# Latent attention with two passes over v, division ahead of the transposes, and column parts in turn

## The chip, the cores and the metric

One core of a Trainium2 chip runs the whole program. The metric is device time in microseconds (us), from the runs of the kernel; beside it stands one profiled execution, from which all details come. The core has a matrix engine (TensorE, PE in the profile, with its weight loads as PEld), a vector engine (VectorE, DVE), a scalar engine (ScalarE, ACT), a general engine (GpSimd, POOL) and a queue that issues transfers (SyncE, SP). The matrix engine writes to PSUM, whose 2 KB banks hold 512 float32 columns; the rest lives in SBUF.

## The reference

Four layers work on 512 latent tokens and 256 context tokens, each 1024 wide. The layers' token mixers are, in order: Fourier mixing, differential attention, latent attention (MLA) and Fourier mixing. Each is followed by a dense layer of 4096 squared-ReLU units. Each sub-layer is preceded by an RMS norm with shift and scale and followed by a gate. After the second layer only the latent stream is updated, so that the third and fourth layers compute 512 columns where the first two compute 768.

```python
def mla_attend(q_nope, q_rope, k_nope, k_rope, v):
    scale = (MLA_NOPE_DIM + MLA_ROPE_DIM) ** -0.5
    s = (jnp.einsum("bqhd,bkhd->bhqk", q_nope, k_nope)
         + jnp.einsum("bqhr,bkr->bhqk", q_rope, k_rope)).astype(jnp.float32) * scale
    p = jax.nn.softmax(s, axis=-1)
    return jnp.einsum("bhqk,bkhe->bqhe", p.astype(v.dtype), v)
...
def sq_relu_mlp(h, w1, w2):
    return jnp.square(jax.nn.relu(h @ w1)) @ w2
```

The latent attention has 16 heads of 64 + 32 (rotary) for the scores and 64 for the values; its queries come from a normalised compression of 256, keys and values from one of 128, and all heads share one rotary key. Each of the 512 latent queries attends to 768 keys.

## The kernel before

All is float32. A product of two float32 operands is made of three matmuls: each operand is split into a high part, rounded for the matrix engine, and a low part, the rest (`split`, L95: ACT copies, DVE subtracts), and high by high, high by low and low by high are added in PSUM. `mm3g` (L147) is that product over k tiles. In it the column parts are the innermost loop: with 768 columns each pair of operands is used for 512 columns and then, at once, for 256 or 258.

**Dense layers** (`mlp`, L394). Per layer there are 32 units `w1(m)` (L413): one load of 128 x 1024 weights, a product over eight k tiles with all columns, and squared ReLU. After each four units comes `w2(j)` (L439): output products over four k tiles for the eight rows of x, accumulated into x by DVE (`accum`, L368, with priority 200). The norm's factor is not applied to the operand: h holds x times the scale (high and low), two more columns hold the shift, and DVE multiplies each unit's result by the factor `r_all` while ACT adds the shift's product `bt`. For 512 tokens the columns are cut into 256 and 256 + 2. While a layer runs, DVE makes the next layer's modulation sums (`mod_unit`, L257).

**Latent attention** (`mla`, L1056). First the three compressions, their norms (`lat_norm`, L1092) and the rotary key (`kr_part`, L1126) are made. The PSUM has two buffers `s` of 1024 columns and four `u` of 512. The loop runs over 32 chunks c: half a head's queries, two row tiles i of 128 queries. For a row tile `S(i)` (L1242) makes 128 x 768 scores, DVE the maximum, and ACT the exponential `e`. `Tr(i)` (L1259) transposes e in two groups of three blocks through a `u` buffer each; each group is split (ACT copies to `pth`, DVE subtracts to `ptl`). `PV(c)` (L1267) multiplies by v: 18 matmuls of 256 columns (v high by `pth`, v low by `pth`, v high by `ptl`), where `vt` holds 64 columns of v beside 64 columns of ones, so that the other 64 rows of the result are the row sums; ACT makes their reciprocal (Ln, then Exp) and DVE multiplies. S runs two row tiles ahead of Tr.

Between the row tiles `fill` (L1232) takes items from a queue, each with a written cost in ns: projections of the next heads (`v_item`, `k_item`, `q_item`, `qr_item`) and output products `wo_item` (L1206), eight for each group of two head pairs, six matmuls of 512 columns each, and one accumulation into x. The rotary parts of q and k are copied to their place under the other 64 rows by ACT and DVE (`kk_rope`, L1143; `q_item`, L1193). Weight splits are ACT's and DVE's (`wload`, L99; `gload`, L111). The last group's output products close the layer, each followed by `MlpNorm.feed` (L341): two scaled copies for the dense layer, and a square that POOL adds to `nacc`.

The order on the matrix engine is the program's order (L48). On the other engines a planner sets the order from estimated costs and priorities. Every engine's queue is served in order.

## Time and profile before

| | |
|---|---|
| runs | 2914.56, 2922.34, 2925.98 us, median 2922.34 |
| profiled execution | 2923.1 us, of which the span from first to last instruction is 2921.0 |
| PE, PEld | 2774.7 us (95%), 2443.5 us (84%) |
| DVE, ACT, POOL | 1949.3 us (67%), 1296.0 us (44%), 159.8 us (5%) |
| mean granted clock of the matrix engine | 0.982 |
| DMA | 291.30 MB, mean 100 GB/s |

Busy times overlap within an engine: a matmul's row covers its whole way through the array, and the next one starts before it ends. Where a text says how far apart two matmuls are, it means their starts. The first dense layer runs from about 178 to 700 us, the second from 1221 to 1742, latent attention from 1758 to 2103, the third dense layer from there to 2452, and the fourth from 2553 to 2900. "Idle before" in a group is the time in which its engine did nothing ahead of its instructions, and the name behind it is what ended that.

### The profile page before, as it was taken

The numbers are of one execution on the slowest core, as the hardware profiler recorded it, in microseconds if no ns is written. First come the engines' busy times: TensorE is split into PE (matmuls) and PEld (weight loads), VectorE is DVE, ScalarE is ACT, GpSimd is POOL, SyncE is SP. The second block draws the span as 40 slices with busy tenths as digits, with TensorE's granted clock in tenths as the row PEclk, the third lists the DMA queues.
The fourth block names the chain that finished last, engine by engine and source line by source line (L and its number), as shares of the span: only waits on it lengthen the run. The fifth ranks groups of instructions, "written<-read, shape, count | busy, mean of one in ns | idle before, by whom it ended". The sixth has DMA issues, their size and how long they took to land.

```text
span 2921.0 us, 42412 instructions
## 1 busy us (share of the span) xinstructions
PE 2774.7 (95%) x16875; PEld 2443.5 (84%) x16875; DVE 1949.3 (67%) x3468; ACT 1296.0 (44%) x2309; POOL 159.8 (5%) x172
## 2 busy tenths in 40 slices
PE   8999999999799898899999998899899999999998
PEld 5788888888788777688888896788799898899997
DVE  8986656558687778874555458888776656544454
ACT  4542222234475656433222246777534335543342
POOL 0100000002110010100000010000100001100001
PEclk9999999999899999999999999999999999999999
DMA  9454333232111111343333211010265541232231
GB/s 326 145 173 131 113 110 108 101 106 71 47 48 45 40 48 44 101 158 114 112 122 108 80 37 37 17 37 23 98 212 168 175 148 55 92 104 94 80 109 51
DMA packets 93542, 291.30 MB, mean 100 GB/s; under 512 B 10624, under 2 KB 14880, under 8 KB 92832
## 3 DMA queue, kind: packets, MB, share of 16 engines
q1 hardware_dynamic: 90784, 285.44, 29.5%
q0 software_dynamic: 2560, 3.15, 0.5%
q8 instruction: 133, 2.18, 0.3%
q14 instruction: 65, 0.53, 0.1%
HBM read 283.29 MB, written 2.11 MB: 98 GB/s over the span
## 4 chain that ended last, share of the span: by engine, by line
PE 79%; DVE 13%; ACT 4%; DMA 2%; issue 1%; POOL 1%; POOLq 0%; SPq 0%; ACTq 0%; DVEq 0%
PE pw L140 69%; PE pu L140 5%; PE ps L140 3%; PE pu L770 1%; DVE x L371 1%; DVE ptl L97 1%; DVE mx L921 1%; DVE hlo L330 1%; DVE nu L328 1%; DMA raw<-in_modw 1%; DVE wlo L97 1%; DVE mx L1253 1%; ACT e L1256 1%; PE pn L140 0%; POOL nacc L357 0%
## 5 line engine op out<-in xcount | busy, mean ns | idle before, releaser
L96 ACT CAST whi<-raw 128x1024 fp32r<-128x1024 f32 (+1 forms) x322 | 312.3, 985 | 1059.7 <-PE pw L140 1010.4
L371 DVE SCALAR_TENSOR_TENSOR x<-pw,mod,x 128x512 f32<-128x512 f32 (+1 forms) x504 | 302.6, 623 | 322.1 <-PE pw L140 321.2
L140 PE MATMUL pw<-hhi,wlo 128*128 128x512 f32 (+1 forms) x2112 | 501.9, 314 | 12.3 <-DVE wlo L97 12.3
L140 PE MATMUL pw<-hhi,whi 128*128 128x512 f32 (+1 forms) x2112 | 502.1, 314 | 5.3 <-ACT whi L96 3.6
L140 PE MATMUL pw<-hlo,whi 128*128 128x512 f32 (+1 forms) x2112 | 501.8, 314 | 0.0
L140 PE MATMUL pw<-ahi,wlo 128*128 128x512 f32 (+1 forms) x1664 | 500.0, 344 | 0.0
L140 PE MATMUL pw<-ahi,whi 128*128 128x512 f32 (+1 forms) x1664 | 496.6, 342 | 0.3 <-DVE x L371 0.3
L140 PE MATMUL pw<-alo,whi 128*128 128x512 f32 (+1 forms) x1664 | 494.9, 341 | 0.0
L97 DVE TENSOR_TENSOR wlo<-raw,whi 128x1024 fp32r<-128x1024 f32 (+1 forms) x322 | 361.6, 1139 | 43.5 <-ACT whi L96 39.0
L140 PEld LDWEIGHTS pw<-hhi,wlo 128*128 128x128 f32 x2112 | 332.6, 190 | 36.4 <-DVE wlo L97 13.0
L140 PEld LDWEIGHTS pw<-hhi,whi 128*128 128x128 f32 x2112 | 333.7, 190 | 32.9 <-ACT whi L96 4.0
L140 PEld LDWEIGHTS pw<-hlo,whi 128*128 128x128 f32 x2112 | 332.6, 190 | 23.4
L140 PEld LDWEIGHTS pw<-ahi,whi 128*128 128x128 f32 x1664 | 284.1, 189 | 41.4 <-DVE x L371 0.8
L140 PEld LDWEIGHTS pw<-ahi,wlo 128*128 128x128 f32 x1664 | 282.7, 189 | 36.6
L140 PEld LDWEIGHTS pw<-alo,whi 128*128 128x128 f32 x1664 | 281.1, 188 | 38.0
L264 DVE SCALAR_TENSOR_TENSOR raw<-raw,cb 128x1024 f32<-128x1024 f32 x176 | 216.0, 1228 | 93.0 <-DMA raw<-in_modw 91.3
L97 DVE TENSOR_TENSOR alo<-r,ahi 128x768 fp32r<-128x768 f32 (+2 forms) x134 | 105.9, 793 | 85.5 <-ACT ahi L96 85.3
L431 ACT ACTIVATE r<-r,bt 128x512 f32<-128x512 f32 (+1 forms) x196 | 119.1, 640 | 78.9 <-DVE r L427 78.9
L264 DVE SCALAR_TENSOR_TENSOR junk<-raw,cb 128x1024 bf16<-128x1024 f32 x96 | 117.2, 1221 | 50.7 <-DMA raw<-in_modw 47.6
L420 DVE COPY bt<-pw 128x2 f32<-128x2 f32 x128 | 20.2, 158 | 195.3 <-PE pw L140 195.1
L307 POOL TENSOR_TENSOR nacc<-nacc,nsq 128x256 f32<-128x256 f32 x70 | 52.9, 755 | 1766.2 <-ACT nsq L306 1765.9
L97 DVE TENSOR_TENSOR ptl<-pu,pth 128x384 fp32r<-128x384 f32 (+1 forms) x208 | 106.3, 540 | 37.4 <-ACT pth L96 35.8
(322 smaller groups left out, 4277.9 us busy)
## 6 DMA issues: line engine op xcount, KB each, us to landing
raw<-in_w SPq DMA_DIRECT2D x252, 512.0 KB, 3.8
raw<-in_modw SPq DMA_DIRECT2D x176, 512.0 KB, 3.4
wm<-in_msh SPq DMA_DIRECT2D x32, 256.0 KB, 6.0
raw<-in_fw SPq DMA_DIRECT2D x10, 512.0 KB, 4.6
cb<-scr SPq DMA_DIRECT2D x4, 1024.0 KB, 4.5
raw<-in_dwk SPq DMA_DIRECT2D x16, 256.0 KB, 2.6
raw<-in_dwq SPq DMA_DIRECT2D x16, 256.0 KB, 2.8
raw<-in_dwv SPq DMA_DIRECT2D x16, 256.0 KB, 2.7
```

The costliest lines, as they stand in the source:

```text
L96: nc.scalar.copy(hi, src)
L97: nc.vector.tensor_sub(lo, src, rd(hi))
L140: r = nc.tensor.matmul(o, lhsT, rhs, start=start, stop=stop)
L264: nc.vector.scalar_tensor_tensor(o, m, 1.0, cb[:, v * 1024:(v + 1) * 1024], op0=ALU.mult, op1=ALU.mult, accum_out=mcol(mod[l, ch], v, k))
L307: nc.gpsimd.tensor_tensor(nacc[:, c0:c0 + w], nacc[:, c0:c0 + w], s, op=ALU.add)
L328: nc.vector.scalar_tensor_tensor(u, xs, am, r, op0=ALU.mult, op1=ALU.mult)
L330: nc.vector.scalar_tensor_tensor(lo, u, sh, rd(hi), op0=ALU.add, op1=ALU.subtract)
L371: nc.vector.scalar_tensor_tensor(xs, src, mcol(mod[l, ch], 0 if c0 < SL else 1, n), xs, op0=ALU.mult, op1=ALU.add)
L431: nc.scalar.activation(r[:, c0:c1], r[:, c0:c1], AF.Relu, bias=bt[:, v:v + 1])
L770: nc.tensor.transpose(t[:, i * 128:(i + 1) * 128], p[:, (k0 + i) * 128:(k0 + i + 1) * 128], ident)
L921: nc.vector.reduce_max(mx, sv, axis=AX.X, negate=True)
L1253: nc.vector.reduce_max(mx, s[:, :T], axis=AX.X)
```

## The change

In `mm3g` and `lin_part` the loop over column parts becomes the outer one: all products of the first part, then all of the next.

In the dense layers of 512 tokens, units from the sixth on (`late`) use an h that has been normalised meanwhile: `normed(k)` makes x times scale times `r_all`, plus the shift, and splits it again into the same tiles, while the first block of output products runs. These units take 24 matmuls of 512 columns in place of 48 of 256 and 258, and ACT applies ReLU straight from PSUM; the multiplication by `r_all` and the copy `bt` are gone.

In the latent attention:

- `vt` holds 64 columns of v's high part beside 64 of its low part. PV has two passes, `pth` and `ptl`, of six matmuls each; the two halves of the result are added.
- The division comes first: ACT's exponential also gives the row sum, DVE its reciprocal, and POOL multiplies the 128 x 768 tile. The scale of the scores goes into the query norm's factor `qg`.
- Six transposes fill one tile `t` of 1024 columns, of which there is one, and it is split 768 wide. `u` has two buffers. S runs three row tiles ahead (`LEAD`).
- The rotary parts are moved by transfers on SP's queue.
- Output products take four head pairs at once, 12 matmuls each; the first half's stand in the loop's last half, the second half's at the end, where the first four are made for three pairs ahead of and behind the last PV, and the fourth pair is added after. Their weights, and those of later projections, are split by ACT and POOL (`sub=`).
- At the start k and v are projected and normalised ahead of q; the four rotary key tiles are all made ahead of the loop. The costs in `fill` differ by quarter.

```diff
     def mm3g(o, n, wfn, afn, parts, off=0):
-        for k in range(n):
-            (wh, wl), (ah, al) = wfn(k), afn(k)
-            for i, (w, v) in enumerate(((wh, ah), (wh, al), (wl, ah))):
-                for c0, w_ in parts:
+        for c0, w_ in parts:
+            for k in range(n):
+                (wh, wl), (ah, al) = wfn(k), afn(k)
+                for i, (w, v) in enumerate(((wh, ah), (wh, al), (wl, ah))):
                     mm(o[:, c0 - off:c0 - off + w_], w, v[:, c0:c0 + w_],
                        k == 0 and i == 0, k == n - 1 and i == 2)
                     yield cost(w_)
...
+            wide = T == SL
+            late = CH + 1 if wide else FF
...
+                if m >= late:
+                    mm3(p, KT, lambda k: kview(w, k), lambda k: h[k], [(0, T)])
+                    step = 256 if m == CH * NJ - 1 else T
+                    for o in range(0, T, step):
+                        s = slice(o, o + step)
+                        nc.scalar.activation(r[:, s], p[:, s], AF.Relu)
+                        nc.scalar.activation(r[:, s], r[:, s], AF.Square)
+                        split(hi[:, s], lo[:, s], r[:, s])
+                    tick()
+                    return hi, lo
...
+            def normed(k):
+                u = rp.tile([128, T], F32, name="cu", tag="cu", bufs=2)
+                hi, lo = (q[:, 0:T] for q in h[k])
+                sh = mcol(mod[l, SH_M], 0, k)
+                nc.vector.scalar_tensor_tensor(
+                    u, x[k][:, 0:T], mcol(amul[l, SC_M], 0, k), r_all, op0=ALU.mult, op1=ALU.mult)
+                nc.scalar.activation(hi, u, AF.Identity, bias=sh)
+                nc.vector.scalar_tensor_tensor(lo, u, sh, rd(hi), op0=ALU.add, op1=ALU.subtract)
...
-            phase(es, "a", 2, {"s": (1024, 2), "u": (512, 4)}, {"t": 1, "v": 1, "r": 1})
+            phase(es, "a", 2, {"s": (1024, 2), "t": (1024, 1), "u": (512, 2)}, {"t": 1, "v": 1, "r": 1})
...
-                nc.scalar.copy(k_h[64:96, :T], rd(krh))
-                nc.vector.tensor_copy(k_l[64:96, :T], rd(krl))
+                nc.sync.dma_start(rd(k_h)[64:96, :T], rd(krh))
+                nc.sync.dma_start(rd(k_l)[64:96, :T], rd(krl))
...
+            def wo_part(p, g, n, k0, k1):
+                w = WO[g, n // 2]
+                for k in range(k0, k1):
+                    (wh, wl), (oh, ol) = w(2 * k + n % 2), O[4 * g + k]
+                    for i, (u, v) in enumerate(((wh, oh), (wh, ol), (wl, oh))):
+                        mm(p, u, v, k == 0 and i == 0, k == 3 and i == 2)
...
-                nc.vector.reduce_max(mx, s[:, :T], axis=AX.X)
-                nc.vector.tensor_scalar(mx, mx, -MLA_SCALE, None, op0=ALU.mult)
-                et = sp.tile([128, T], F32, name="e", tag="e", bufs=3)
-                nc.scalar.activation(et, s[:, :T], AF.Exp, bias=mx, scale=MLA_SCALE)
+                li = sp.tile([128, 1], F32, name="li", tag="li", bufs=4)
+                nc.vector.reduce_max(mx, s[:, :T], axis=AX.X, negate=True)
+                et = sp.tile([128, T], F32, name="e", tag="e", bufs=4)
+                nc.scalar.activation(et, s[:, :T], AF.Exp, bias=mx, accum_out=li)
+                nc.vector.reciprocal(li, li)
+                nc.gpsimd.tensor_scalar(et, et, li, None, op0=ALU.mult)
...
-                pth, ptl = PT[c]
-                for b in range(2):
-                    transpose_g(e, pth, ptl, qi * 128, 3 * b, 3, "u")
+                transpose_g(e, *PT[c], qi * 128, 0, 6)
...
+                for i, pt in enumerate((pth, ptl)):
                     for kt in range(6):
-                        for vv, pt in ps:
-                            mm(o, vv[:, kt, bl:bl + 2].rearrange("p b e -> p (b e)"), pt[:, kt], i == 0, i == 17)
-                            i += 1
+                        mm(o, vt[:, kt, hd % 4].rearrange("p q e -> p (q e)"), pt[:, kt], i + kt == 0, i + kt == 6)
                 s, sl = slice(64 * b, 64 * b + 64), slice(64 - 64 * b, 128 - 64 * b)
                 u = nt_("u")
-                nc.scalar.activation(u[s], o[sl], AF.Ln)
-                nc.scalar.activation(u[s], u[s], AF.Exp, scale=-1.0)
-                nc.vector.tensor_mul(u[s], o[s], u[s])
+                nc.scalar.copy(u[s], o[sl])
+                nc.vector.tensor_add(u[s], o[s], u[s])
...
+            LEAD = 3
+            st = {i: S(i) for i in range(LEAD)}
...
-                    fill(1050.0, 2 if g == 3 else 0)
-                if m == 0:
-                    need(f"wo{g - 2}")
-                PV(c)
-            ahead_w1(l)
+                    fill((560.0, 460.0, 1300.0, 1000.0)[g])
+                if c == NC - 4:
+                    need("wo0")
+                    wo_load(1, 0)
+                    wo_load(1, 1)
+                if c < NC - 1:
+                    PV(c)
...
+            p0, p1 = pt_("s"), pt_("s")
+            ps = [p0[:, 0:512], p0[:, 512:1024], p1[:, 0:512], p1[:, 512:1024]]
+            for n in range(2):
+                wo_part(ps[n], 1, n, 0, 3)
+            PV(NC - 1)
+            for n in range(2, 4):
+                wo_part(ps[n], 1, n, 0, 3)
+            wo_load(1, 2)
+            ahead_w1(l)
             for n in range(KT):
-                wo_item(3, n, nm)
+                if n < 4:
+                    wo_part(ps[n], 1, n, 3, 4)
+                else:
+                    ps.append(pt_("u"))
+                    wo_part(ps[n], 1, n, 0, 4)
+                accum(n, 0, SL, ps[n], l, G_A)
+                if n == 1:
+                    wo_load(1, 3)
+                nm.feed(n)
```

More of the change, by code (lines that the diff above doesn't have):

```diff
@@ L105, in wload, with gload @@
         lo = pl.tile([128, wd], F32R, name="wlo", tag="w")
-        split(hi[:, :n], lo[:, :n], raw[:, :n])
+        split(hi[:, :n], lo[:, :n], raw[:, :n], sub)
         return hi, lo
     pre = {}
-    def gload(srcs, n=512):
+    def gload(srcs, n=512, sub=None):
         w = []
@@ L117, in gload @@
             hi, lo = (gp.tile([128, 512], F32R, name="g", tag="g", bufs=4) for _ in range(2))
-            split(hi[:, :n], lo[:, :n], raw[:, :n])
+            split(hi[:, :n], lo[:, :n], raw[:, :n], sub)
             w.append((hi, lo))
@@ L415, in w1 @@
                 p = pt_("w")
+                r = rp.tile([128, T], F32, name="r", tag="r", bufs=2)
+                hi = ap_.tile([128, T], F32R, name="ahi", tag="a")
+                lo = ap_.tile([128, T], F32R, name="alo", tag="a")
+                if m >= late:
[8 more added lines that the diff above has]
+                    return hi, lo
                 mm3(p, KT, lambda k: (kview if m else hview)(w, k), lambda k: h[k], hparts, off=-po)
@@ L420, in w1 @@
                 nc.vector.tensor_copy(bt, p[:, po + T:po + T + 2])
-                r = rp.tile([128, T], F32, name="r", tag="r", bufs=2)
-                hi = ap_.tile([128, T], F32R, name="ahi", tag="a")
-                lo = ap_.tile([128, T], F32R, name="alo", tag="a")
                 step = 256 if m == CH * NJ - 1 else T
@@ L442, in w2 @@
                 if j < NJ - 1:
-                    run(out_gemm_g(CH, wfn, lambda k: act[k], T, l, G_M))
+                    run(out_gemm_g(CH, wfn, lambda k: act[k], T, l, G_M, before=normed if wide and j == 0 else None))
                     return
@@ L510, in lin_part @@
     def lin_part(p, w, Y, k0, k1, T):
-        for k in range(k0, k1):
-            (wh, wl), (yh, yl) = (hview if type(w) is list else kview)(w, k), Y[k]
-            for i, (u, v) in enumerate(((wh, yh), (wh, yl), (wl, yh))):
-                for c0, w_ in parts(T):
+        for c0, w_ in parts(T):
+            for k in range(k0, k1):
+                (wh, wl), (yh, yl) = (hview if type(w) is list else kview)(w, k), Y[k]
+                for i, (u, v) in enumerate(((wh, yh), (wh, yl), (wl, yh))):
                     mm(p[:, c0:c0 + w_], u, v[:, c0:c0 + w_], k == 0 and i == 0, k == KT - 1 and i == 2)
@@ L1202, in q_item, with wo_load, wo_item @@
                     s = slice(32 * (hd % 4), 32 * (hd % 4) + 32)
-                    nc.scalar.copy(qh[64:96], rd(qr[hd // 4][0][s]))
-                    nc.vector.tensor_copy(ql[64:96], rd(qr[hd // 4][1][s]))
-            def wo_item(g, n, norm=None):
+                    nc.sync.dma_start(rd(qh)[64:96], rd(qr[hd // 4][0][s]))
+                    nc.sync.dma_start(rd(ql)[64:96], rd(qr[hd // 4][1][s]))
+            def wo_load(g, b):
+                if b >= 4:
+                    return
+                if (g, b) != (1, 2):
+                    w = wload(wp, a["mwo"][g, b], sub=nc.gpsimd)
+                    WO[g, b] = lambda i: kview(w, i)
+                    return
+                ws = []
+                for src in halves_of(a["mwo"][g, b]):
+                    raw = rawt()
+                    nc.sync.dma_start(raw[:, :512], src)
+                    ws.append([sp.tile([128, 512], F32R, name=q, tag="o", bufs=14) for q in ("woh", "wol")])
+                    split(*ws[-1], raw[:, :512])
+                WO[g, b] = lambda i: hview(ws, i)
+            def wo_part(p, g, n, k0, k1):
+                w = WO[g, n // 2]
+                for k in range(k0, k1):
+                    (wh, wl), (oh, ol) = w(2 * k + n % 2), O[4 * g + k]
+                    for i, (u, v) in enumerate(((wh, oh), (wh, ol), (wl, oh))):
+                        mm(p, u, v, k == 0 and i == 0, k == 3 and i == 2)
+            def wo_item(g, n):
                 if n == 0:
-                    WO[g] = [wload(wp, a["mwo"][2 * g + i]) for i in range(2)]
+                    wo_load(g, 0)
+                if n % 2 == 0:
+                    wo_load(g, n // 2 + 1)
                 p = pt_("u")
-                mm3(p, 2, lambda k: kview(WO[g][k], n), lambda k: O[2 * g + k], parts(SL))
+                wo_part(p, g, n, 0, 4)
                 accum(n, 0, SL, p, l, G_A)
-                if norm:
-                    norm.feed(n)
             def v_items(g):
@@ L1222, in wo_items @@
             def wo_items(g):
-                return [(f"wo{g}", 1300, wo_item, g, n) for n in range(KT)]
+                return [(f"wo{g}", 2700, wo_item, g, n) for n in range(KT)]
             queue, debt = [], [0.0]
@@ L1270, in PV @@
                 if c0 == 0 and b == 0:
-                    O[pr] = [sp.tile([128, 512], F32R, name=n, tag="o", bufs=8) for n in ("oh", "ol")]
+                    O[pr] = [sp.tile([128, 512], F32R, name=n, tag="o", bufs=14) for n in ("oh", "ol")]
                 oh, ol = O[pr]
```

99 lines of the change are left out of this document (48 added, 51 removed).

## The prediction

> **What bounds the kernel now.** The views were read in this order: the table of stretches, the order of matmuls in time, the groups by shape inside the attention loop, the chain that ended last at both ends of that layer. The table first (us; PE, weight-load, DVE, ACT and POOL busy, granted clock, DMA share, GB/s):
>
> ```profile
> core 0: us, PE busy (x) PEld busy (x) DVE busy (x) ACT busy (x) POOL busy (x), PEclk, DMA share, GB/s
> 1758.00:1810.00 52.00, 43.52 (x200) 32.88 (x200) 43.26 (x82) 33.57 (x66) 4.14 (x5) 0.90 0.10 37
> 1810.00:2071.00 261.00, 243.21 (x1601) 215.97 (x1602) 216.85 (x437) 187.95 (x374) 4.14 (x3) 0.99 0.08 27
> 2071.00:2103.00 32.00, 26.18 (x135) 21.47 (x134) 24.60 (x40) 17.31 (x35) 12.42 (x7) 0.93 0.18 64
> 2553.00:2900.00 347.00, 347.00 (x2297) 320.52 (x2295) 165.67 (x230) 128.76 (x174) 5.74 (x8) 1.00 0.26 88
> ```
>
> The last row is a dense layer (the fourth): TensorE is busy from end to end at full clock, so time there is the number of matmuls times their spacing. The latent attention is the three rows ahead of it: a start of 52 us (PE 43.5), a loop of 261 us (PE 243, DVE 217), an end of 32 us.
>
> Since PE's busy time overlaps from one matmul to the next, the price of a matmul is the distance between starts. First and last rows of undisturbed runs (start, length, engine, line, what; "x2" is two matmuls of one name):
>
> ```profile
> 399.78 0.51 PE L140 MATMUL pw<-hhi,wlo 128*128 128x512 f32 x2
> ...
> 411.74 0.51 PE L140 MATMUL pw<-hhi,whi 128*128 128x512 f32 x2
> ...
> 425.50 0.51 PE L140 MATMUL pw<-ahi,whi 128*128 128x512 f32 x2
> ...
> 432.56 0.52 PE L140 MATMUL pw<-ahi,wlo 128*128 128x512 f32 x2
> ...
> 684.80 0.28 PE L140 MATMUL pw<-ahi,wlo 128*128 128x256 f32 x1
> ...
> 695.24 0.28 PE L140 MATMUL pw<-ahi,wlo 128*128 128x256 f32 x1
> ...
> 1765.23 0.39 PE L140 MATMUL ps<-hlo,whi 128*128 128x512 f32 x1
> ...
> 1775.88 0.39 PE L140 MATMUL ps<-hhi,wlo 128*128 128x512 f32 x1
> ...
> 2699.83 0.40 PE L140 MATMUL pw<-hlo,whi 128*128 128x256 f32 x2
> ...
> 2710.12 0.40 PE L140 MATMUL pw<-hhi,wlo 128*128 128x256 f32 x2
> 2710.36 0.40 PE L140 MATMUL pw<-ahi,whi 128*128 128x512 f32 x1
> ...
> 2731.92 0.39 PE L140 MATMUL pw<-ahi,wlo 128*128 128x512 f32 x1
> ```
>
> Divided by their counts these give: 512+258 columns in turn on h, 34 pairs, 0.3518 a pair; 512+256 in turn on the activations, 20 pairs, 0.3530; 256 alone, 87, 0.1200; 512 alone on h, 46, 0.2315; 256+258 in turn on h, 43 pairs, 0.2393; 512 alone on the activations, 95, 0.2269.
>
> **Column parts.** In the two 768-wide dense layers all 512-column products of an output tile now come ahead of the narrow ones. Second GEMM: 0.2269 + 0.1200 = 0.3469 for 0.3530 a pair, 0.0061 x 672 pairs (7 x 8 x 12) = 4.1 us a layer. First GEMM, whose operand h gave 0.2315: 0.2315 + 0.1197 (half of 0.2393) = 0.3512 for 0.3518, x 768 = 0.5 us. So 4.6 a layer, 9.2 for two. Bounds: if 512-wide costs 0.2315 on both operands, 1.5 a layer; if 0.2269 on both, 8.1. The first layer's 192 linear pairs give 0.3 more (0 to 1.2).
>
> **Late units of the 512-wide dense layers.** 27 of 32 first-GEMM units take 24 matmuls of 512 on a normalised h for 48 of 256 and 258: (0.2393 - 0.2315) x 24 x 27 = 5.1 us a layer, 10.1 for two; with 0.2269, 8.0 a layer. The eight `normed` steps add two 512-wide DVE operations each (0.74, the x row below) and an ACT one, 11.9 us of DVE under the first block of output products, 96 x 0.2269 = 21.8 us. DVE is busy 15.67 of these in the third layer:
>
> ```profile
> 2125.70:2147.50 21.80, 21.80 (x108) 18.49 (x107) 15.67 (x25) 5.22 (x8) 0.00 (x0) 1.00 0.66 216
> ```
>
> 15.7 + 11.9 exceeds 21.8 by 5.8, so the next unit could start that late; I take 0, since the modulation sums in that sum can wait, and keep 6 as the bound. Dense layers together: 9.2 + 0.3 + 10.1 = 19.6 saved, bounds 5 and 33.
>
> **The attention loop.** Groups between 1810 and 2071 (busy, mean ns | idle before):
>
> ```profile
> L97 DVE TENSOR_TENSOR ptl<-pu,pth 128x384 fp32r<-128x384 f32 x125 | 64.0, 549 | 34.2 <-ACT pth L96 33.6
> L1253 DVE TENSOR_REDUCE mx<-ps 128x1 f32<-128x768 f32 x62 | 58.6, 948 | 1.3 <-PE ps L140 0.8
> L371 DVE SCALAR_TENSOR_TENSOR x<-pu,mod,x 128x512 f32<-128x512 f32 x22 | 16.4, 744 | 0.5
> L97 DVE TENSOR_TENSOR ol<-nu,oh 64x256 fp32r<-64x256 f32 x30 | 12.5, 416 | 0.6
> L1204 DVE CAST ql<-qrl 32x512 fp32r<-32x512 f32 x14 | 5.9, 420 | 0.4
> L1256 ACT ACTIVATE e<-ps,mx 128x768 f32<-128x768 f32 x64 | 57.5, 903 | 36.1 <-DVE mx L1254 35.7
> L96 ACT CAST pth<-pu 128x384 fp32r<-128x384 f32 x127 | 55.2, 480 | 6.0 <-PE pu L770 5.0
> L770 PE MATMUL pu<-ident,e 128*128 128x128 f32 x383 | 56.2, 279 | 16.2 <-ACT e L1256 12.2 <-DVE ptl L97 1.9 <-DVE kkl L97 1.8
> ```
>
> PE work goes down. Value products: 6 x 0.12 less for each of 31 in the loop, 22.3 us. Output products: 132 matmuls were in the loop, 96 are, so 36 x 0.2269 = 8.2 us move to the end. 243.2 - 30.5 = 212.7. Of the 18 us in which PE is idle, 12.2 wait for `e`; a third score tile in flight covers that (the POOL product and ACT's accumulator read come on top, 0.86 and 0.2 below). Were the rest alone left, the loop would take 212.7 + 5.8 = 218.5. DVE also drops: one 768-wide subtraction (0.95, as the 768-wide reduction) for two of 0.549 gives 64 x 0.15 = 10, the rotary casts 6, 14 of 22 accumulations 10, weight splits some 10: about 181, no bound.
>
> What is new is that six transposes fill one buffer that exists once, where three fill one of four. A row tile now, in order of time:
>
> ```profile
> 1830.44 0.82 PE L770 MATMUL pu<-ident,e 128*128 128x128 f32 x6
> ...
> 1831.02 0.60 PE L140 MATMUL ps<-kkh,qh 96*128 96x512 f32 x2
> 1831.03 0.86 ACT L96 CAST pth<-pu 128x384 fp32r<-128x384 f32 x2
> ...
> 1831.54 1.02 DVE L97 TENSOR_TENSOR ptl<-pu,pth 128x384 fp32r<-128x384 f32 x2
> ...
> 1832.16 0.72 PE L140 MATMUL pu<-cqn,whi 128*128 128x512 f32 x2
> ```
>
> The halves overlap: 2.12 us from the first transpose to the end of the second subtraction, with no wait for the buffer. PE needs 0.58 for the transposes and 1.14 for the scores. Undivided, the steps follow each other: 0.82, ACT copy 0.80 (two of 0.480 less one start), DVE 0.95, handovers 0.1, and a wait on each in-order queue; ACT (188 of 261) and DVE (217 of 261) are mostly busy with other operations of up to 0.95, so some 0.25 each. Cycle 3.2 us. Without filler PE is at the next transposes after 1.72, so it waits. In the odd half of a chunk the value products follow (12 x 0.12 = 1.44): six on the high part, ready at 0.82 + 0.25 + 0.80 + 0.05 = 1.9, six after 3.2, end at about 4.0. Chunk without filler: 3.2 + 4.0 = 7.2; projections of up to 1.4 us fit in the gaps. In the third quarter six chunks carry an output product of 12 x 0.2269 = 2.72 in the even half: 0.58 + 1.14 + 2.72 + 4.0 = 8.4. The quarters: 8 x 7.2 = 57.6 each for the first two, say 58 for what does not fit; 6 x 8.4 + 2 x 9 (projections of v, k, q) = 68.4; the fourth 57.6 + 2 x 1.2 for two output products + 2 for projections - 1.4 (the last value product leaves the loop) = 60.6. Sum 245, against 261: 16 saved. Bounds: 218.5 above (42.5 saved), and the ring at its worst (third rival).
>
> **Early division.** The product on POOL has no row; the nearest are a one-input cast of 768 elements and a two-input addition of 768, and ACT's accumulator read stands in the attention before it:
>
> ```profile
> L812 POOL CAST kl<-big 64x768 fp32r<-64x768 f32 x4 | 3.4, 857 | 0.2
> L357 POOL TENSOR_TENSOR nacc<-nacc,big 128x768 f32<-128x768 f32 x7 | 13.3, 1897 | 76.8 <-ACT big L356 66.7 <-ACT hhi L96 9.9
> L922 ACT ACTIVATION_READ_ACCUMULATOR e<-ps,mx 128x1 f32 x58 | 11.3, 195 | 0.0
> ```
>
> One input: I take 0.86, 64 x 0.86 = 55 us on an engine that is idle in the loop; 1.90 gives 122. From the scores to a divided tile: 1.14 + 0.95 + 0.90 + 0.20 + 0.15 + 0.86 = 4.2, or 5.2, inside three row tiles (3 x 3.6 = 11), so it costs nothing while POOL's queue is short; weight subtractions of some 2.5 us (1.90 x 1024/768) that now stand in that queue are covered by the same slack. The Trainium skill's page "GPSIMD Engine Reference" (4.1 Engine selection) calls one-input work there roughly line-rate, against half of DVE's speed for two inputs; the two rows agree with it, and by it 0.86 is right; no run here shows the operation itself.
>
> **Start.** PE is idle 8.5 of 52 us and runs partly at half clock (0.90 in the row). k and v are projected and normalised ahead, and the rotary copies leave ACT and DVE for SP's queue, where eight transfers of key parts and four for each head pair stand among the weight loads; the first scores wait for a landing instead. The nearest row is a 256 KB load (us to landing last):
>
> ```profile
> raw<-in_dwk SPq DMA_DIRECT2D x16, 256.0 KB, 2.6
> ```
>
> These carry 64 to 96 KB; I take 2, which the value and key projections between cover in part. One score tile more comes ahead. I take 4 saved; bounds 3 lost (the landing stays bare) and 9.
>
> **End.** Rows of before:
>
> ```profile
> 2081.96 0.15 DVE L97 TENSOR_TENSOR hlo<-mod,hhi 128x2 fp32r<-128x2 f32 x1
> ...
> 2086.06 0.55 DVE L97 TENSOR_TENSOR hlo<-mod,hhi 128x2 fp32r<-128x2 f32 x1
> ...
> 2084.78 12.89 POOL L357 TENSOR_TENSOR nacc<-nacc,nsqw 128x512 f32<-128x512 f32 x7 [245.56 <-ACT hhi L96]
> ...
> 2097.70 0.33 SPq L103 DMA_DIRECT2D raw<-in_w  x1
> ...
> 2102.47 0.80 PE L140 MATMUL pw<-hhi,whi 128*128 128x256 f32 x2 [3.62 <-ACT whi L96]
> ```
>
> Seven POOL additions of 1.84 each end at 2097.67, the second dense weight is requested only then (as if its buffer had been the squares'), and PE is at full rate 4.8 later: 31 us from the last transposes, with which the loop's row ends. Now: 18 products (4.1), the last value product (1.4), 18 more (4.1), then the last quarter of four outputs (2.7) and four whole ones (10.9), the last accumulated and squared (1.4), one POOL addition (1.8), and 4.8: 31.2. Nothing, though 8.2 us of PE work came here from the loop. If the weight split on POOL falls between the additions, 2.5 later.
>
> **Sum.** The profiled execution took 2923.1 (span 2921.0), the runs' median is 2922.34, so the sum may stand for either. 2923.1 - 19.6 - 16 - 4 - 0 = 2883.5.
>
> **Rivals.** *The ring is hidden* (planner puts the splits first; fillers fall well): the loop is 218.5, 2923.1 - 19.6 - 42.5 - 4 = 2857. For it: 33.6 us of DVE's idle stands at exactly these splits. Against: the gaps have few fillers in the first half of the loop.
>
> *Alternation costs nothing* (the distance belongs to operand and width): dense layers save the lower 5 only, 2898. For it: 512 on h stands at 0.2315 alone too.
>
> *POOL and DVE hinder each other.* In the rows above a two-column subtraction with both inputs in SBUF takes 0.15 alone and 0.55 while POOL adds. The subtraction `ol` (0.416, both inputs in SBUF) would wait for POOL's product, and the split behind it in DVE's queue with it. With products of 1.90 and half of one to wait for at each chunk, the chunk is 0.95 longer, the loop 30: 245 + 30 = 275, 14 more than before, and 2923.1 - 19.6 - 4 + 14 = 2913.5; with every second one met, 2898.5. Against: at 0.86 a product there is half as much to meet. The Trainium skill's page "SBUF — State Buffer" (Who interferes with whom) has that rule, that a DVE instruction with two SBUF inputs contends with a GpSimd one that reads SBUF and one with a PSUM input does not. The rows agree with its first half; by its second the 768-wide split, which reads PSUM, stays free.
>
> *The ring decides, slower.* If each split finds its engine in a whole 0.95 operation, the cycle is 0.82 + 0.95 + 0.80 + 0.95 + 0.95 + 0.1 = 4.6 and the odd half 5.4: 10.0 a chunk, 320 - 1.4 for the loop, 57.6 longer. 2923.1 - 19.6 - 4 + 57.6 = 2957. It makes the kernel slower from a chunk of (261 + 23.6 + 1.4) / 32 = 8.9 us on. For it: two engines over 70% busy and strict queues. Against: the present splits show waits of a quarter of that.
>
> **How the numbers follow.** Chances: forecast 0.46 (own range 2868 to 2900), ring hidden 0.27, alternation 0.10, POOL 0.10, slower ring 0.07. The forecast is 2884; the range 2840 to 2922 takes in the hidden ring with the dense layers at their best (2857 - 13 = 2844) and POOL's case with half of what the dense layers may lose (2913.5 + 7). A measurement here can tell 0.5% (14.6 us): faster below 2907.7, slower above 2936.9. Forecast, hidden ring, alternation and two fifths of POOL's case (the shorter waits) are faster: 0.87; the rest of POOL's case is the same: 0.06; slower 0.07.
>
> **What would show it.** Right: 512-wide distances near 0.227 to 0.232 and no 0.353 pair in the dense layers; 24 matmuls in late units; PE in the loop waiting at transposes for the subtraction `ptl`, no longer for `e`; chunks near 7.2 us, and near 8.4 in the third quarter. Wrong: dense layers of unchanged length; the loop's chunks above 8.9; transposes that wait for POOL; an end that grows past 31 us.

## The result and the profile after

The changed kernel takes 2954.14 us (median) beside 2918.45 before: ratio 1.0116, 95% interval 1.0094 to 1.0137. It is slower by 1.2%; the forecast was 2884, with a range of 2840 to 2922. The dense layers became faster as the change has it; the latent attention became 44 us longer. Table of stretches of the kernel after (columns as in the prediction): start, loop, end of the latent attention, and the fourth dense layer.

```profile
1754.90:1816.80 61.90, 48.52 (x206) 36.23 (x206) 41.89 (x79) 28.70 (x58) 5.89 (x6) 0.86 0.19 51
1816.80:2106.70 289.90, 233.76 (x1374) 200.61 (x1375) 195.09 (x336) 170.70 (x329) 164.35 (x78) 0.92 0.10 30
2106.70:2168.90 62.20, 55.86 (x356) 49.83 (x355) 44.85 (x70) 29.75 (x52) 11.82 (x8) 0.97 0.42 143
2615.00:2942.00 327.00, 326.90 (x1520) 271.89 (x1519) 145.47 (x180) 116.05 (x166) 9.13 (x13) 1.00 0.26 84
```

With the same borders (first query product, first transposes, last transposes, first output product of the third dense layer) the kernel before has 52.3, 260.8 and 56.9. No engine is full in the loop, and TensorE's mean clock is 0.92 where it was 0.99. What it waits for there (us in total, times, longest):

```profile
PE pt L800 <- DVE ptl L98: 32.0, 21, 3.5
PE pu L143 <- DVE vt L98: 9.4, 5, 2.4
PE pu L143 <- DVE kkl L98: 8.4, 9, 2.3
PE pu L143 <- ACT pth L96: 4.1, 3, 2.8
...
PE pt L800 <- POOL e L1309: 1.0, 1, 1.0
```

The scores' exponential, 12.2 us before, is gone from the list. In its place stand the one tile `t` and the projections that want a buffer `u` (`vt`, `kkl`). The wait for POOL, 1.0, ends just where the loop begins and is not counted as idle time of the loop below. The half clock comes on top. One stretch of 3.4 us after a wait, with the 6.8 us ahead of it:

```profile
1943.30:1950.10 6.80, 4.77 (x34) 3.99 (x33) 6.00 (x11) 5.43 (x11) 4.49 (x3) 1.00 0.08 19
1950.10:1953.50 3.40, 3.40 (x16) 3.11 (x15) 1.81 (x2) 0.80 (x1) 2.11 (x1) 0.51 0.00 0
```

TensorE stood still for 2.0 of the 6.8 us, and the next 3.4 us ran at half clock (the clock changes on borders 3.41 us apart). All 11 such stretches in the loop have 1.7 to 3.8 us of idle time in the 6.8 us ahead.

So a loop can be taken apart, roughly, into work at full clock, idle time, and half of its time at half clock. For every kernel of this study (us, from the traces; the ratio is to the kernel before):

| kernel | start | loop | idle | at half clock | end | ratio of times |
|---|---|---|---|---|---|---|
| before | 52.3 | 260.8 | 17.4 | 7.6 | 56.9 | 1 |
| after | 61.9 | 289.9 | 56.1 | 44.6 | 62.2 | 1.0116 |
| e1_dense | 52.1 | 261.7 | 17.6 | 10.5 | 55.9 | 0.9962 |
| e2_u4 | 58.5 | 253.2 | 33.3 | 24.5 | 63.5 | 0.9996 |
| e3_t2 | 62.0 | 264.3 | 44.0 | 30.8 | 60.6 | 1.0050 |
| e4_nodiv | 60.7 | 274.5 | 51.0 | 18.7 | 64.1 | 1.0090 |
| e9_noprod | 60.6 | 279.0 | 48.4 | 36.6 | 63.8 | 1.0070 |
| e5_actrec | 62.9 | 299.5 | 59.8 | 64.5 | 62.2 | 1.0145 |
| e13_rope | 62.0 | 279.7 | 53.6 | 24.3 | 62.2 | 1.0100 |
| e15_alone | 62.1 | 279.6 | 53.6 | 24.1 | 62.3 | 1.0096 |
| e6_halves | 62.5 | 289.2 | 57.0 | 40.7 | 61.8 | 1.0109 |
| e7_u4ha | 53.4 | 259.8 | 38.2 | 24.4 | 62.4 | 0.9976 |
| e8_u4han | 54.5 | 258.7 | 35.7 | 26.6 | 65.5 | 0.9990 |
| e10_two3 | 55.0 | 273.0 | 37.9 | 37.8 | 55.2 | 1.0000 |
| e11_two4 | 57.5 | 253.6 | 28.4 | 21.5 | 59.3 | 0.9945 |
| e12_two4s | 56.3 | 268.2 | 36.1 | 32.7 | 55.8 | 0.9999 |
| e14_two4b | 52.5 | 234.5 | 17.1 | 6.8 | 58.2 | 0.9898 |

One of the four runs of e14_two4b took 5850 us and is not in its time. From before to after: 30.5 less work (the prediction's count), 38.7 more idle time, 18.5 more from the clock ((44.6 - 7.6) / 2): 26.7 of the 29.1 that were measured.

### The profile page after: what moved, and what is told of

Read it like the earlier page. It is cut to its first block, busy times and chain, and to the rows that moved or that the text cites. A ratio compares the mean times of both kernels' runs of the same rounds, so it can differ in the third digit from the quotient of the medians.

```text
span 2956.0 us, 39518 instructions
## 1 busy us (share of the span) xinstructions
PE 2760.7 (93%) x15387; PEld 2370.3 (80%) x15387; DVE 1904.7 (64%) x3279; ACT 1267.1 (43%) x2270; POOL 320.6 (11%) x248
## 4 chain that ended last, share of the span: by engine, by line
PE 75%; DVE 14%; ACT 4%; DMA 4%; issue 2%; POOL 1%; POOLq 0%; SPq 0%; ACTq 0%; DVEq 0%
PE pw L143 64%; PE pu L143 5%; PE ps L143 4%; DVE x L374 1%; PE pt L800 1%; DVE ptl L98 1%; DVE mx L951 1%; DVE raw L267 1%; DMA raw<-in_modw 1%; DVE wlo L98 1%; DMA raw<-in_w 1%; DVE junk L267 1%; DVE hlo L333 1%; DVE nu L331 1%; POOL e L1309 1%
## 5 line engine op out<-in xcount | busy, mean ns | idle before, releaser
L143 PE MATMUL pw<-hhi,wlo 128*128 128x512 f32 (+2 forms) x1680 | 587.2, 350 | 13.0 <-DVE wlo L98 13.0
L143 PE MATMUL pw<-hhi,whi 128*128 128x512 f32 (+2 forms) x1680 | 590.7, 352 | 3.7 <-ACT whi L96 2.0
L143 PE MATMUL pw<-hlo,whi 128*128 128x512 f32 (+2 forms) x1680 | 589.4, 351 | 0.0
L143 PE MATMUL pw<-ahi,whi 128*128 128x512 f32 (+1 forms) x1664 | 569.8, 342 | 2.3 <-DVE x L374 1.8
L143 PE MATMUL pw<-alo,whi 128*128 128x512 f32 (+1 forms) x1664 | 568.5, 342 | 1.0 <-DVE alo L98 1.0
L143 PE MATMUL pw<-ahi,wlo 128*128 128x512 f32 (+1 forms) x1664 | 567.2, 341 | 0.0
L143 PEld LDWEIGHTS pw<-hhi,wlo 128*128 128x128 f32 x1680 | 318.7, 190 | 56.9 <-DVE wlo L98 13.6
L143 PEld LDWEIGHTS pw<-alo,whi 128*128 128x128 f32 x1664 | 316.0, 190 | 37.2 <-DVE alo L98 1.6
L1309 POOL TENSOR_SCALAR e<-e,li 128x768 f32<-128x768 f32 x64 | 141.0, 2204 | 126.2 <-DVE li L1308 91.7
L143 PE MATMUL pw<-hhi,g 128*128 128x512 f32 (+2 forms) x384 | 96.3, 334 | 3.9 <-DVE x L374 2.9
L453 ACT ACTIVATE r<-r,bt 128x512 f32<-128x512 f32 (+1 forms) x140 | 79.7, 613 | 47.0 <-DVE r L449 41.9
```

The source lines that it names most:

```text
L143: r = nc.tensor.matmul(o, lhsT, rhs, start=start, stop=stop)
L453: nc.scalar.activation(r[:, c0:c1], r[:, c0:c1], AF.Relu, bias=bt[:, v:v + 1])
L1309: nc.gpsimd.tensor_scalar(et, et, li, None, op0=ALU.mult)
```

## The experiments

### The dense layers alone (e1_dense)

The kernel before with `mm3g`, `lin_part`, `out_gemm_g` and `mlp` of the changed kernel; of the diff:

```diff
-        for k in range(n):
-            (wh, wl), (ah, al) = wfn(k), afn(k)
-            for i, (w, v) in enumerate(((wh, ah), (wh, al), (wl, ah))):
-                for c0, w_ in parts:
+        for c0, w_ in parts:
+            for k in range(n):
+                (wh, wl), (ah, al) = wfn(k), afn(k)
+                for i, (w, v) in enumerate(((wh, ah), (wh, al), (wl, ah))):
...
+            late = CH + 1 if wide else FF
```

> The kernel before with the column parts in turn (dense layers, Fourier products, differential attention) and the late units and `normed` of the 512-wide dense layers; the latent attention is left as it was. By the stretches of the two traces (dense layers 1.4 + 2.9 + 0.3 + 4.9 us shorter, Fourier mixing 1.0) it should be 10.5 us faster than before, 0.4%: about 2908 beside 2918. By the prediction's own sum for these parts it would be 19.6 faster, 2899. If the column parts cost or gain nothing: 2918. What is missing to 2954 lies in the latent attention in each case.

Measured: 2907.23, ratio 0.9962 (0.9947 to 0.9977), 11 us faster. Between first and last output product the four dense layers took 499.3, 497.9, 327.6 and 326.0, where before they took 500.9, 500.9, 331.2 and 331.0. The expected total of 10.5 was met, though the third layer gave 3.6 where 0.3 was expected; the forecast's 19.6 was too much. The rest of the change therefore costs 46 us.

### Buffers: the tile `t` and the number of `u` (e2_u4, e3_t2)

In e2_u4 the tile `t` goes, and the transposes stand in two groups through `u`; in e3_t2 the same groups go through a `t` of `(512, 2)`, and `u` stays at `(512, 2)`.

```diff
-phase(es, "a", 2, {"s": (1024, 2), "t": (1024, 1), "u": (512, 2)}, ...)
+phase(es, "a", 2, {"s": (1024, 2), "u": (512, 4)}, ...)
-                transpose_g(e, *PT[c], qi * 128, 0, 6)
+                for b in range(2):
+                    transpose_g(e, *PT[c], qi * 128, 3 * b, 3, "u")
```

> The changed kernel with the transposes again in two groups of three through the buffers `u`, of which there are four again; no tile `t`. Theory A (one tile `t` and two `u` make TensorE wait, and the waits bring the half clock): the waits ahead of transposes (40 us) and of projections and value products (34) shrink to the size of before, the loop falls from 290 to about 245, granted clock near 0.98, time about 2909. Theory B (POOL's product or its weight splits are late): loop stays near 285, time 2945 to 2955. Theory C (the order of the projections, by their written costs): the same as B.

> The changed kernel with two tiles `t` of 512 columns in place of one of 1024: the transposes are split 384 wide and the halves overlap; `u` stays at two. It parts theory A in two. If the one tile `t` that holds all six transposes is what costs: transposes no longer wait for `ptl` (32 us of such waits fall under 8), loop 250 to 260, time 2915 to 2925. If two `u` are what costs: loop 275 to 285, time 2940 to 2950, and waits of projections for DVE stay. Theories B and C: no change, 2950 to 2955.

e2_u4: 2916.55, ratio 0.9996 (0.9987 to 1.0006); the loop fell by 36.7, where theory A had 45. e3_t2: 2933.46, 1.0050 (1.0033 to 1.0067); the loop fell by 25.6, which lies between its two cases. Loop and largest waits of e3_t2, then loop and largest wait of e2_u4:

```profile
1815.70:2080.00 264.30, 220.25 (x1374) 192.51 (x1375) 197.56 (x398) 173.72 (x393) 165.02 (x78) 0.94 0.11 30
PE pu L143 <- DVE kkl L98: 14.7, 7, 3.4
PE pt L800 <- POOL e L1309: 8.4, 7, 2.2
PE pt L800 <- DVE ptl L98: 4.5, 6, 0.8
```

```profile
1817.20:2070.40 253.20, 219.91 (x1373) 191.35 (x1374) 201.71 (x400) 172.07 (x393) 165.61 (x78) 0.95 0.11 31
PE pu L800 <- POOL e L1309: 15.6, 9, 4.6
```

Two half tiles take the wait for `ptl` from 32.0 to 4.5; four `u` then take 11 us more. Theory A is borne out as the larger part. The two kernels use the same four banks of PSUM; in e2_u4 any of them may serve transposes and projections, and there the chunks with projections are 25 us shorter in all, the others 12 us longer (the table of chunks below). What comes to light underneath is POOL's product. The changed costs in `fill` (theory C) were not tried by themselves.

### The division (e4_nodiv, e9_noprod, e5_actrec, e13_rope, e15_alone)

e4_nodiv leaves out both of these lines, e9_noprod only the second; e5_actrec has the ACT lines in place of the first:

```diff
-                nc.vector.reciprocal(li, li)
-                nc.gpsimd.tensor_scalar(et, et, li, None, op0=ALU.mult)
...
+                nc.scalar.activation(li, li, AF.Ln)
+                nc.scalar.activation(li, li, AF.Exp, scale=-1.0)
```

e13_rope changes one line of `rope`; e15_alone takes away `sub=nc.gpsimd` as well:

```diff
-                nc.gpsimd.tensor_tensor(s, s, sin[0:n], op=ALU.mult)
+                nc.vector.tensor_mul(s, s, sin[0:n])
```

> The changed kernel without the reciprocal and POOL's product: the exponentials are not divided at all (this part of the computation is left out). Theory B: the 141 us of POOL's products are gone, and the loop falls by 20 us or more, time under 2935. Theory A: the divided tile was 2 to 13 us early at its transposes, so leaving it out changes nothing: loop 285 to 290, time 2948 to 2955.

> The changed kernel without POOL's product, but with DVE's reciprocal (the exponentials are not divided: this part of the computation is left out; the reciprocal is made and not used). It parts the 15 us of loop that went when both were left out. If the product costs them: loop 273 to 278, half-clock stretches as few as there (5 for 11), time 2940 to 2944. If the reciprocal in DVE's queue costs them: loop 285 to 291, time 2950 to 2957.

> The changed kernel with the reciprocal of the row sum made by ACT (Ln, then Exp with scale -1, right behind the exponential) in place of DVE; POOL's product stays. Leaving out both reciprocal and product shortened the loop by 15 us. If it is the reciprocal, which stands in DVE's in-order queue and waits there for ACT's exponential (10.1 us busy and 15.4 us idle ahead of it), the loop falls from 290 to 275 to 280, time 2939 to 2945. If it is POOL's product (141 us on POOL, 2.2 each): loop 286 to 292, time 2950 to 2957, or longer, since ACT has 128 small operations more.

> The changed kernel with the rotary embedding's product with the sine made by DVE in place of POOL (four such in the layer, three in the loop). Without POOL's division product the loop was 11 us shorter, and row tile by row tile these 11 us arise at three places beside the three sine products (2.4, 2.5 and 3.4) and at one beside POOL's first two weight subtractions (3.8). If the product costs through POOL's queue, because DVE waits in order for the sine product that stands behind two divisions: the first three places go, loop 281 to 284, time about 2946. If the division itself slows other engines: loop 289 to 291, time 2953 to 2956.

> The kernel of e13_rope with the weights of the loop split by DVE too, so that POOL does nothing in the loop but the divisions. If POOL's queue is the only way in which the division costs: loop 277 to 281, as without the product, less what DVE's 22 us of added subtractions cost (0 to 4): 278 to 285, time 2941 to 2948. If the division itself costs: loop 289 or more.

e4_nodiv took 2941.64 (1.0071 to 1.0109), loop 274.5: the expectation that a product which is early costs nothing was wrong. e9_noprod took 2940.36 (1.0053 to 1.0087), loop 279.0: most of it is the product, not the reciprocal. e5_actrec, the reciprocal on ACT, took 2963.18 (1.0130 to 1.0160), loop 299.5: by the trace, ACT's added operations cost more than the reciprocal on DVE; the intervals of the times overlap the kernel after. In e9_noprod every engine does the rest in the same order as after, so the two can be laid side by side: the 11 us arise beside the sine products of the rotary embedding and POOL's first weight subtractions, and nowhere in the second half of the loop. One such place in the kernel after, DVE and then POOL (start, length, engine, line; times in brackets are waits):

```profile
1842.66 0.69 DVE L1103 TENSOR_TENSOR rt<-rt,rsw 128x512 f32<-128x512 f32 x1 [1.18 <-POOL rsw L1102]
1843.27 0.95 DVE L1305 TENSOR_REDUCE mx<-ps 128x1 f32<-128x768 f32 x1
...
1846.51 0.95 DVE L98 TENSOR_TENSOR ptl<-pt,pth 128x768 fp32r<-128x768 f32 x1
```

```profile
1836.89 4.50 POOL L1309 TENSOR_SCALAR e<-e,li 128x768 f32<-128x768 f32 x2 [0.40 <-PE ps L143]
1841.35 1.28 POOL L1102 TENSOR_TENSOR rsw<-rsw,msin 128x512 f32<-128x512 f32 x1
```

Two divisions of 2.2 us stand ahead of the sine product; DVE waits 1.18 us for it, and behind DVE's waiting addition stand a row maximum and the next split. With that product on DVE (e13_rope) the loop is 279.7:

```profile
1813.90:2093.60 279.70, 226.05 (x1373) 192.94 (x1374) 196.79 (x339) 170.07 (x329) 160.61 (x75) 0.96 0.11 31
```

That is 10.2 us less, mostly by the clock (idle 2.5 less, time at half clock 20.3 less); taking the weights off POOL as well (e15_alone, 279.6) adds nothing. In the runs' times e13_rope stands at 1.0100 (1.0080 to 1.0120) and e15_alone at 1.0096 (1.0079 to 1.0113), which overlap the kernel after; the difference rests on the traces. A second pair agrees: e6_halves below, whose loop is that of the kernel after, has 289.2, e15_alone 279.6.

### The two ends (e6_halves, e7_u4ha) and POOL's weights (e8_u4han)

e6_halves has the edits below; e7_u4ha joins it with e2_u4 and e5_actrec; e8_u4han is e7_u4ha without `sub=nc.gpsimd`.

```diff
-            mm3(pkv, KT, lambda k: kview(wkv, k), hk, [(512, 256)])
+            pkc = pt_("u")[:, :256]
+            mm3(pkc, KT, lambda k: kview(wkv, k), hk, [(512, 256)], off=512)
...
+            for n in range(4):
+                wo_part(ps[n], 1, n, 3, 4)
             for n in range(KT):
-                if n < 4:
-                    wo_part(ps[n], 1, n, 3, 4)
-                else:
+                if n >= 4:
```

> The changed kernel with two edits, one at each end: the compression's 256 context columns go to a buffer `u` of their own, not into the second half of the PSUM tile whose first half the norm still reads; at the end the four last quarters of output products are all issued ahead of the first accumulation, so that none writes into the second half of a tile whose first half DVE is adding. If these halves of one tile, which are waited for as a whole, cost the ends their 15 us: the start falls from 61.9 to about 56.5 (a wait of 5.5 us gone) and the end from 62.2 to about 60 (1.0 and 1.4), time about 2946. If the new order as such costs (rotary transfers, items that wait for each other): both unchanged, 2954.

> The kernel of e2_u4 (384-wide splits through four `u`) with the edits of e5_actrec and e6_halves together. If the three causes add: 2916.5 less 7 (ends) less 3 to 8 (reciprocal, where DVE waits 13 us for it): 2901 to 2907. If the reciprocal only counts in the ring of the one tile `t`: 2908 to 2911.

> The kernel of e7_u4ha with the weights of the loop split by DVE as before, not by POOL (12 subtractions, 22 us of POOL in the loop). In e2_u4 the largest wait left was TensorE's at transposes for POOL's product (15.6 us), which stood behind such subtractions, and these behind ACT's copies. If that is so: the waits fall under 5, loop 8 to 12 shorter than in e7_u4ha, time about 2893 to 2897. If DVE (202 of 253 us busy, then about 215) is what the split then waits for: the same as e7_u4ha within 4 us.

e6_halves: 2951.57 (1.0094 to 1.0124), start 62.5, end 61.8: neither edit gained. e7_u4ha: 2912.28 (0.9967 to 0.9985), just outside both of its cases, start 53.4. Largest wait of the start in the kernel after, in e6_halves and in e7_u4ha:

```profile
PE ps L143 <- DVE u L1130: 5.0, 1, 5.0
```

```profile
PE pu L143 <- DVE v L288: 4.8, 2, 3.7
```

```profile
PE ps L143 <- DMA qh<-qrh: 4.5, 1, 4.5
```

With a buffer of its own but only two `u`, the wait moves to the norm that holds the other `u`. With four, the start is 8.5 shorter and the landing of the rotary part lies bare. The loop of e7_u4ha is 6.6 longer than e2_u4's, again with the reciprocal on ACT. e8_u4han: 2916.72 (0.9980 to 0.9999), loop 1 us shorter only, though TensorE's waits for POOL's product fell from 23.9 to 18.7: what the weight subtractions cost on POOL, DVE seems to pay in their place (its busy time in the loop rose from 196 to 206).

### The two passes alone (e10_two3, e11_two4, e12_two4s, e14_two4b)

The three edits below belong to e11_two4, e12_two4s and e14_two4b. e10_two3 is e1_dense with `vt`, `S` and `PV` of the changed kernel and `LEAD = 3`; e11_two4 has `LEAD = 4` and five tiles `e`; e12_two4s shares the product; e14_two4b is e11_two4 with `MLA_SCALE` in `qg`, and with rotary parts by transfers for all head pairs but the first.

```diff
-            st = {0: S(0)}
-            st[1] = S(1)
+            LEAD = 4
+            st = {i: S(i) for i in range(LEAD)}
...
-                nc.gpsimd.tensor_scalar(et, et, li, None, op0=ALU.mult)
+                nc.vector.tensor_scalar(et[:, 512:T], et[:, 512:T], li, None, op0=ALU.mult)
+                nc.gpsimd.tensor_scalar(et[:, 0:512], et[:, 0:512], li, None, op0=ALU.mult)
...
-                    nc.scalar.copy(qh[64:96], rd(qr[hd // 4][0][s]))
-                    nc.vector.tensor_copy(ql[64:96], rd(qr[hd // 4][1][s]))
+                    if pr == 0:
+                        nc.scalar.copy(qh[64:96], rd(qr[hd // 4][0][s]))
+                        nc.vector.tensor_copy(ql[64:96], rd(qr[hd // 4][1][s]))
+                    else:
+                        nc.sync.dma_start(rd(qh)[64:96], rd(qr[hd // 4][0][s]))
+                        nc.sync.dma_start(rd(ql)[64:96], rd(qr[hd // 4][1][s]))
```

> The kernel of e1_dense (column parts and late units; latent attention as before) with only the early division and the two passes over v added, and the scores three row tiles ahead; start, end, output products of two head pairs, four `u` and 384-wide splits stay as before. TensorE has 22 us less to do in a loop of 261.6. If waits for POOL's product (15.6 us in e2_u4) eat most of it: loop 255 to 262, time 2900 to 2907. If the product is hidden: loop 240 to 246, time 2886 to 2892.

> The kernel of e10_two3 with the scores four row tiles ahead and five tiles `e`. In e2_u4 a divided tile was ready 7.3 us after its scores on the mean (up to 14.4) and needed 9.6 after them. If that chain is what TensorE waits for, a row tile more (some 3.9 us) covers it: loop 6 to 12 shorter than in e10_two3. If DVE and ACT are the bound, the same within 2 us.

> The kernel of e11_two4 with the product shared: POOL multiplies the first 512 columns, DVE the last 256. POOL's 2.2 us fall to about 1.5 a row tile; DVE has some 64 x 0.3 = 19 us more. If POOL's product is still late in e11_two4: faster by up to 5 us. If DVE is the tighter: slower by up to 10.

> The kernel of e11_two4 with the change's relief for DVE and ACT: the scale of the scores in the query norm's factor (one small DVE operation a row tile less), and the rotary parts moved by transfers, but only those that are needed inside the loop. If DVE (226 of 254 us busy) is the bound there: loop 4 to 8 shorter, time 2896 to 2900. If the two score tiles are (TensorE waits 13.4 us for ACT's exponential to free one): the same within 2 us, or 1 to 3 shorter.

e10_two3: 2919.10, ratio 1.0000 (0.9990 to 1.0009); the loop is 11 us longer than e1_dense's, with 22 us less work, and longer than either case of the expectation. e11_two4: 2903.96, 0.9945 (0.9929 to 0.9961), its loop 19 us shorter where 6 to 12 were expected. e12_two4s: 2918.57, 0.9999 (0.9988 to 1.0010), 15 us slower where 10 was the limit: DVE, now busy for 248 of 268 us, is the tighter engine. e14_two4b: 2887.59, 0.9898 (0.9873 to 0.9923), faster than both kernels. Waits of e10_two3, then loop and largest wait of e14_two4b:

```profile
PE ps L140 <- ACT e L1279: 14.3, 10, 4.3
PE pu L797 <- POOL e L1281: 14.3, 17, 1.7
```

```profile
1809.90:2044.40 234.50, 217.36 (x1403) 191.98 (x1404) 212.58 (x420) 171.82 (x390) 148.07 (x66) 0.99 0.11 32
PE ps L140 <- ACT e L1289: 6.4, 5, 1.6
```

A score tile more covers the product (the wait for POOL falls from 14.3 to 4.0 in e11_two4). With DVE at 213 us in place of 226, both the idle time (28.4 to 17.1) and the half clock (21.5 to 6.8) fall: 19 us where 4 to 8 were expected, since the clock's share, 7.3, was in no expectation.

## Why the prediction was wrong

From the sum, 2883.5, to the profiled execution, 2957.74, it is 74 us: 45 in the loop, 14 at the start, 5 at the end and 10 in the dense layers.

**Column parts: right, one term too large.** The distances came out as forecast; rows of the first and the fourth dense layer after:

```profile
242.02 0.40 PE L143 MATMUL pw<-alo,whi 128*128 128x512 f32 x1
...
244.31 0.39 PE L143 MATMUL pw<-ahi,wlo 128*128 128x512 f32 x1
...
2739.06 0.39 PE L143 MATMUL pw<-hhi,wlo 128*128 128x512 f32 x1
...
2743.46 0.39 PE L143 MATMUL pw<-hhi,whi 128*128 128x512 f32 x1
```

Ten distances of 0.229 on the activations, nineteen of 0.2316 on h, no pair of 0.353. But 0.2269, taken over from the 512-wide layers, measures 0.2290 in the 768-wide ones: (0.3530 - 0.2290 - 0.1200) x 672 = 2.7 in place of 4.1 on the second GEMM. Measured were 3.0 in the second layer and 1.5 in the first, where 4.6 were forecast, with 1.5 to 8.1 as bounds.

**Late units: right.** 4.9 in the fourth layer for 5.1. In the third, 3.6 in e1_dense and 0.3 in the kernel after, where one wait and its clock cost what is missing:

```profile
2230.17 1.22 DVE L267 SCALAR_TENSOR_TENSOR raw<-raw,cb 128x1024 f32<-128x1024 f32 x1 [3.92 <-DMA raw<-in_modw]
...
2231.32 1.40 DVE L374 SCALAR_TENSOR_TENSOR x<-pw,mod,x 128x512 f32<-128x512 f32 x2
...
2232.12 0.51 PE L143 MATMUL pw<-ahi,whi 128*128 128x512 f32 x1 [1.83 <-DVE x L374]
```

DVE waits for the landing of a modulation weight, the accumulation that frees TensorE's buffer stands behind it, and from 2233.5 to 2236.9 the clock is 0.50: 1.8 + 1.7 us. In e1_dense DVE waits up to 3.8 us for such landings too, without holding TensorE; why they meet here stays open. `normed` was not what it waited for.

**The loop: the ring was priced right, the filler and the clock were not.** A row tile from the first transpose to the end of `ptl` takes 3.24 us on the mean, forecast 3.2. PE's work at full clock is 289.9 - 56.1 - 22.3 = 211.5, forecast 212.7. Whole chunks by what they hold (mean us, number; the last, part of a chunk, is left out):

| | projections | output product | neither |
|---|---|---|---|
| forecast | 7.7, what its sum leaves (14) | 8.4 (7) | 7.2 (10) |
| before | 9.68 (12) | 7.75 (13) | 7.02 (6) |
| after | 10.41 (14) | 8.15 (7) | 8.38 (10) |
| e13_rope | 10.10 (14) | 8.15 (7) | 7.79 (10) |
| e3_t2 | 10.26 (14) | 7.65 (7) | 6.35 (10) |
| e2_u4 | 8.44 (14) | 8.07 (7) | 7.24 (10) |
| e14_two4b | 8.79 (12) | 6.92 (13) | 6.29 (6) |

Of the 45 us between 245 and 290, 37 lie in the chunks with projections, 12 in the bare ones (half of it goes with the sine products, as e13_rope's row shows), and the rest of the loop is 4 under. The step that failed is "projections of up to 1.4 us fit in the gaps" and the small allowance for what does not. A projection does not only want TensorE's gap; it wants one of two `u` and turns on ACT and DVE, whose queues already carry the ring. The worst chunk but one, 16.1 us, TensorE, DVE and ACT:

```profile
1967.46 0.95 PE L143 MATMUL pu<-g,ckn 128*128 128x256 f32 x6
1969.03 0.93 PE L143 MATMUL pu<-ckn,g 128*128 128x512 f32 x3 [0.61 <-DVE vt L98]
1972.33 0.59 PE L143 MATMUL pu<-ckn,g 128*128 128x256 f32 x3 [2.36 <-DVE vt L98]
```

```profile
1968.80 0.95 DVE L1305 TENSOR_REDUCE mx<-ps 128x1 f32<-128x768 f32 x1
1969.66 0.41 DVE L98 TENSOR_TENSOR vt<-pu,vt 128x256 fp32r<-128x256 f32 x1
1970.61 0.68 DVE L98 TENSOR_TENSOR kkl<-pu,kkh 64x512 fp32r<-64x512 f32 x1 [0.53 <-ACT kkh L96]
1971.50 0.16 DVE L1308 RECIPROCAL li<-li 128x1 f32<-128x1 f32 x1 [0.21 <-ACT e L1307]
1971.76 0.42 DVE L98 TENSOR_TENSOR vt<-pu,vt 128x256 fp32r<-128x256 f32 x1
```

```profile
1970.48 0.89 ACT L1307 ACTIVATE e<-ps,mx 128x768 f32<-128x768 f32 x1
...
1971.37 0.35 ACT L96 CAST vt<-pu 128x256 fp32r<-128x256 f32 x1
```

The third value projection is computed by 1968.4, but the last subtraction that reads its buffer ends at 1972.2: ahead of it in DVE's queue stand a row maximum, a key part and a reciprocal that waits for ACT. The copy that it needs from ACT ends only at 1971.7, behind an exponential in ACT's queue. TensorE stands for 2.36 us, with the next projections and the value product behind. That a `u` is what the projections lack is shown by e3_t2 and e2_u4: with two tiles `t` but two `u` their chunks still take 10.26 us, with four `u` 8.44. The prediction asked what waits in the ring, not what waits for a `u`. It also counted all time at full clock. Taken by kind, the 45 us are 24 of idle time beyond the forecast's 32 (245 - 212.7) and 22 of half clock, less 1 of work.

**Early division: wrong.** "It costs nothing while POOL's queue is short" took 0.86 us a product:

```profile
L1309 POOL TENSOR_SCALAR e<-e,li 128x768 f32<-128x768 f32 x63 | 138.8, 2204 | 115.8 <-DVE li L1308 81.3 <-PE ps L143 27.7 <-PE pu L143 3.5
L98 DVE TENSOR_TENSOR ol<-nu,oh 64x256 fp32r<-64x256 f32 x31 | 12.8, 414 | 0.7 <-ACT oh L96 0.3
```

It is 2.2, above even the upper bound of 1.90. The tile was still early (by 5.8 us on the mean, with no wait of TensorE for it inside the loop); the queue behind it was not named: the rotary sine product, 10 us of loop by e13_rope's trace. The rival by which POOL and DVE hinder each other at `ol` is not what happened: `ol` takes 0.414 with POOL busy for 164 of 290 us, 0.416 before, and none of the 22 that overlap a division is longer than 0.43. It is not impossible, though: in e2_u4 six of 31 take 0.68 to 2.37 (mean of all 0.569, 5 us of the loop), three of these under POOL's weight subtractions and three under its divisions. The Trainium skill's page "SBUF — State Buffer" (Who interferes with whom) has a DVE instruction with two SBUF inputs contend with a GpSimd one that reads SBUF; the runs show that now and then, not each time. The Trainium skill's page "GPSIMD Engine Reference" (4.1 Engine selection), by which 0.86 seemed right, calls one-input work there roughly line-rate; the row, 2.2 us for 768 elements with a scalar for each partition, does not bear it out.

**Start: wrong.** Four shorter were forecast, 9.6 longer measured: the products into the second half of a PSUM tile waited 5.0 for DVE's reading of the first (e6_halves, above), and with two `u` a buffer of its own only moved that wait. The lower bound's cause, a bare landing, was real too (4.5 in e7_u4ha).

**End: wrong by 5.** Its first stretch and two of its waits:

```profile
2106.70:2110.90 4.20, 4.20 (x14) 3.32 (x13) 0.96 (x1) 0.80 (x1) 0.00 (x0) 0.59 0.02 4
```

```profile
PE ps L143 <- DVE x L374: 2.0, 2, 1.2
PE pw L143 <- ACT whi L96: 2.0, 1, 2.0
```

The first 4.2 us run at a clock of 0.59, and products on the half-ahead tiles wait 2.0 for the accumulation into `x`; neither was in the sum. The wait for ACT's copy of the second dense weight (3.62 before) is still there with 2.0. Moving the quarters ahead changed nothing (61.8), the order with two head pairs takes 55.2 to 59.3.

**Rivals.** The slower ring named the right time, 2957, for a wrong reason: its cycle of 4.6 us is 3.24. That is luck. Its threshold, a mean chunk of 8.9, was passed ((289.9 + 1.4) / 32 = 9.1), but by the projections. The hidden ring is out, with 32.0 us of waits at the transposes, and alternation did cost something: the dense layers gained 13 us by e1_dense's stretches, between its 5 and the forecast's 19.6.
